# Layer 1's keys written by tile in the projection, a late end of attention blocks, and result stores from GpSimd

## The chip, the cores and the metric

The kernel runs on one core of a Trainium2 chip, as one launch. The metric is the device time of that launch in microseconds (us). A core has five engines with in-order instruction streams: TensorE (PE in the profile; its weight loads are listed as PEld), VectorE (DVE), ScalarE (ACT), GpSimd (POOL) and SyncE (SP, which here only issues transfers). A transfer is issued by an engine's queue and carried out by the core's 16 DMA engines.

## The reference

A backbone of two layers over 2048 latent tokens (a grid of 32 rows by 64 columns) of width 1024, with 256 context tokens. All is float32. Layer 0 mixes multi-head latent attention and a gated linear attention and updates both streams; layer 1, which the change is about, is a 2-D neighbourhood attention with 16 heads of 64:

```python
def odd_mixer(h, hc, w_in, q_gain, k_gain, rpb, w_out, update_ctx):
    ...                                   # q, k, v, z = split(h @ w_in); q, k = rms_norm per head
    o = neighborhood_attention(q_x, k_x, v_x, k_c, v_c, rpb)
    y = jnp.dot(o.reshape(...) * jax.nn.silu(z_x), w_out)

def neighborhood_attention(q, k, v, k_ctx, v_ctx, rpb):
    # a query at (row, col) sees a window of 8 rows x 16 columns of latent keys, with a bias
    # by relative place, and all 256 context keys
    s_lat = einsum('bqhd,brkhd->bhqrk', qr, kb) * scale + bias      # masked outside the 16 columns
    s_ctx = einsum('bqhd,bchd->bhqc', qr, k_ctx) * scale
    p = softmax(concatenate([s_lat, s_ctx], axis=-1))
    return p[..., :n] @ vb + p[..., n:] @ v_ctx
```

Each layer ends with `x = x + gate * y`. Products are kept near float32 accuracy by splitting an operand into a high part (type fp32r, which the fast matmul takes) and a low part.

## The kernel before

The work goes through stages one after the other: layer 0's projections, its attentions, its output projection, then layer 1: `odd_qk` (query and key projections), `odd_vz` (value and gate projections, woven with row maxima of the scores), `odd_attention`, and the output projection. Intermediate tensors (Q1, K1, V1, z1, RT1) go to device memory and come back. Instructions are written in program order; a scheduler of the tile framework then orders them on each engine by its own model of time, and `tc.issue_after(x)` adds the constraint that what is issued in its scope comes after x. A tile name with `bufs=n` is a ring of n buffers: the next use of a buffer waits until all readers of the last one are done.

*`odd_qk`.* A `cell` is one 128-token tile times 512 columns: 24 matmuls, the sum of squares, the power by POOL (`rpow`, L197), and the scaling. Its second half, `fin`, runs inside the next cell: four PE transposes (L1133), ACT writes the high part `oqh` (L106 is the helper of all activations), DVE the low part `oql` (L1137), and SP stores both to Q1 or K1 with tokens in row order (L1143). Of a key cell, both parts go to K1.

*`odd_attention`* runs over eight pairs of heads j. A pair goes through 20 steps: c0, c1, l0 to l3, c2, l4 to l7, c3, l8 to l15. A "c" step takes the 256 context keys against 512 queries; an "l" step takes one tile of 128 keys (8 rows by 16 columns) against its rectangle of queries. Four l steps form a group g, which covers 512 keys. A step is:

- the scores: two accumulating matmuls per head and key tile, `scores` (L1321 and L1322). The second one has 65 rows: 64 of the keys' high part against the queries' low part, and a row of ones against the row maxima;
- for l steps, DVE adds the bias table into a probability tile `opt` (L1431); ACT takes the exponential;
- two steps later in a batch of two (the list `pend`), the *tail*: P·V into the block's PSUM tile `o` (L1348 for c, L1363 for l), and the running sums of probabilities `oacc`: DVE adds the two context halves (L1354), POOL adds l tiles (L1371).

The latent queries form four blocks of 512. After steps 7, 11 and 15 the tail ends blocks 0, 1, and 2 with 3: `finish` (L823 to L837) sums `oacc` over partitions with two matmuls (L828) into a PSUM tile of the scores' own ring "st" of four, ACT takes a logarithm and an exponential for the reciprocal, DVE refines it (L833, L834) and multiplies it with `o` (L835), POOL multiplies with the gate `ozt` (L836), and SP stores the result to RT1 (L837). `finish` serves layer 0's attention too.

*Loads.* All are on SP's queue. Per pair: queries (L1281 to L1283, six of 512 KB and two short ones), context keys `kc`, values (L1309 for context, L1311 for eight parts of V1 in rows of 512 bytes), two bias tables (L1316). Per group, `keys` loads 512 keys into the staging tile `kb` (one buffer), 64 partitions at a time: high and low part stacked on 128 partitions (L1293), the high part again (L1294), and a row of ones (L1295). The generator `by_tile` then copies `kb` to `kt` with ACT, from rows of the grid to tiles of 16 columns, 128x512 and 65x512 for each head; one such copy is issued after the last exponential of each l step of the group before. The rings: `st` 4 and `o` 4 in PSUM, `opt` 10, `kt` 2, queries 2.

In the last pair the output weights are loaded and split in the places that queries, values, tables and keys leave (`weights`).

## Time and profile before

| | us |
|---|---|
| median of 3 runs | 3788.31 |
| the three runs | 3780.18, 3788.31, 3790.68 |
| profiled execution | 3781.03 |
| its span in the trace | 3779.2 |
| `odd_qk` | 2205 to 2655 |
| `odd_vz` and row maxima | 2655 to 3111 |
| `odd_attention` | 3111 to 3592 |
| layer 1's output projection | 3592 to 3779 |

All durations are from the profiled execution. Its page gives the busy time of each engine, and the granted clock of TensorE as a mean, 0.979 over the span. A row of a window gives the busy time and, in brackets, the number of instructions that began in it. A row of the timeline gives start, duration, engine, line, operation, output and input, and in square brackets how long the engine had been idle and which other instruction it waited for; "SPq" is the issue of a transfer by SyncE. In a row of the waits the columns are the total, the number and the longest wait. A few per cent of the matmuls can be missing from a trace.

### The profile page before, as it was taken

What the parts mean: (1) busy time and instruction counts of PE and PEld (TensorE: products, weight loads), DVE (VectorE), ACT (ScalarE), POOL (GpSimd) and SP (SyncE); (2) the same over time, 40 slices, a digit from 0 to 9 for tenths busy, and PEclk for the clock granted to TensorE, in tenths of its full rate; (3) what the DMA queues carried; (4) which work ended last, traced back from release to release, by engine and by line L of the source; (5) the groups of instructions that cost most, each with busy time, mean ns of one, the idle gap of its engine ahead of it and who ended that gap; (6) DMA issues with size and microseconds to landing.
All of it is one profiled execution on the core that took longest, in us unless ns stands there. A gap on an engine that the chain in (4) does not pass through costs nothing. (4 is left out here: it accounts for less than half of the span.)

```text
span 3779.2 us, 52751 instructions
## 1 busy us (share of the span) xinstructions
PE 3608.8 (95%) x18404; PEld 2768.6 (73%) x18404; DVE 2368.2 (63%) x4699; ACT 1474.2 (39%) x2932; POOL 1418.8 (38%) x1585
## 2 busy tenths in 40 slices
PE   7999989999999999989999999998999998889899
PEld 6988978888876666645557878887888875545577
DVE  4677656888866666696654344445687745657732
ACT  4445541111135555545552133334222225656610
POOL 1434320010024444445642223333444426766722
PEclk9999999999999999999999999999999998899999
DMA  7455453222252331425515544446444459787543
GB/s 253 138 165 163 130 169 97 70 86 70 76 134 67 85 98 58 115 78 146 144 37 184 162 136 132 128 133 184 152 137 146 118 142 199 197 192 184 158 143 117
DMA packets 373820, 503.03 MB, mean 133 GB/s; under 512 B 29554, under 2 KB 250834, under 8 KB 367651
## 3 DMA queue, kind: packets, MB, share of 16 engines
q1 hardware_dynamic: 339122, 443.55, 41.9%
q0 software_dynamic: 11776, 28.13, 2.4%
q10 hardware_dynamic: 22656, 27.99, 2.1%
q8 instruction: 146, 2.39, 0.3%
q14 instruction: 120, 0.98, 0.1%
HBM read 329.60 MB, written 169.93 MB: 132 GB/s over the span
## 5 line engine op out<-in xcount | busy, mean ns | idle before, releaser
L106 ACT ACTIVATE apt<-st 128x512 f32<-128x512 f32 (+1 forms) x592 | 343.4, 593 | 278.5 <-PE st L963 248.4
L647 DVE TENSOR_REDUCE mm<-mx 128x1 f32<-128x512 f32 (+1 forms) x656 | 389.0, 627 | 82.2 <-PE mx L646 75.1
L952 DVE TENSOR_TENSOR acc<-acc,apt 128x512 f32<-128x512 f32 x288 | 272.9, 971 | 143.2 <-ACT apt L106 141.7
L952 POOL TENSOR_TENSOR acc<-acc,apt 128x512 f32<-128x512 f32 x160 | 227.5, 1435 | 188.8 <-ACT apt L106 188.1
L1371 POOL TENSOR_TENSOR oacc<-oacc,opt 128x341 f32<-128x341 f32 (+7 forms) x336 | 238.7, 742 | 115.3 <-ACT opt L106 80.1
L893 PE MATMUL av<-apt,av 128*64 128x512 f32 (+1 forms) x1184 | 279.1, 595 | 0.1
L961 PE MATMUL st<-aq,akh 97*128 97x512 f32 (+1 forms) x592 | 255.1, 431 | 8.3 <-ACT apt L106 6.2
L646 PE MATMUL mx<-mk,mq 96*128 96x512 f32 (+1 forms) x656 | 236.7, 373 | 6.2 <-DMA mq<-QT 4.7
L962 PE MATMUL st<-aq,akh 96*128 96x512 f32 (+1 forms) x592 | 233.5, 395 | 0.0
L963 PE MATMUL st<-aq,akl 96*128 96x512 f32 (+1 forms) x592 | 232.9, 394 | 0.0
L1239 DVE CUSTOM_DVE_ANT_1 mx<-mx,mtab 128x225 f32<-128x225 f32 (+13 forms) x576 | 183.6, 339 | 58.6 <-PE mx L1233 43.2
L106 ACT ACTIVATE u<-gm 128x352 f32<-128x352 f32 (+1 forms) x140 | 68.7, 498 | 370.2 <-PE gm L125 208.7
L1075 POOL TENSOR_TENSOR px<-py,px 128x512 f32<-128x512 f32 x68 | 89.8, 1321 | 277.0 <-DVE py L1074 274.8
L893 PEld LDWEIGHTS av<-apt,av 128*64 128x64 f32 x1184 | 80.4, 137 | 153.3 <-issue 151.5
L1431 DVE TENSOR_TENSOR opt<-st,tab 128x64 f32<-128x64 f32 (+10 forms) x576 | 144.9, 313 | 70.0 <-PE st L1322 50.5
L1074 DVE TENSOR_TENSOR py<-pj,gate 128x512 f32<-128x512 f32 x68 | 46.9, 690 | 217.6 <-PE pj L116 217.6
L961 PEld LDWEIGHTS st<-aq,akh 97*128 97x128 f32 x592 | 111.8, 189 | 96.0 <-issue 46.8
L106 ACT ACTIVATE opt<-opt 128x465 f32<-128x465 f32 (+7 forms) x256 | 123.0, 497 | 57.0 <-DVE opt L1431 47.3
L646 PEld LDWEIGHTS mx<-mk,mq 96*128 96x128 f32 x656 | 121.7, 189 | 17.7 <-issue 5.1
L106 ACT ACTIVATE prh<-pr 128x1024 fp32r<-128x1024 f32 x34 | 35.7, 1056 | 251.6 <-PE pj L115 251.6
L1321 PE MATMUL st<-q,kt 128*128 128x480 f32 (+5 forms) x256 | 100.9, 404 | 34.4 <-ACT opt L106 17.3
L963 PEld LDWEIGHTS st<-aq,akl 96*128 96x128 f32 x592 | 112.8, 191 | 25.2
(436 smaller groups left out, 10314.4 us busy)
## 6 DMA issues: line engine op xcount, KB each, us to landing
q<-Q SPq DMA_DIRECT2D x48, 512.0 KB
kb<-K SPq DMA_DIRECT2D x192, 128.0 KB
H<-x ACTq DMA_DIRECT2D x36, 512.0 KB
pr<-RT SPq DMA_DIRECT2D x34, 512.0 KB
adaw<-ada_w SPq DMA_DIRECT2D x64, 256.0 KB
x<-H SPq DMA_DIRECT2D x32, 512.0 KB
wraw<-w_od SPq DMA_DIRECT2D x64, 256.0 KB
mtab<-rpb_q SPq DMA_DIRECT2D x16, 899.0 KB
```

Source lines behind the costliest of these rows:

```text
L106: return self.nc.scalar.activation(out, in_, func, **kw)
L646: mm = nc.tensor.matmul(ps[:, :w], q[:A_QK, (t % 6) * P : (t % 6) * P + P], k[:A_QK, k0 : k0 + w], start=True, stop=True)
L647: nc.vector.tensor_reduce(out=m[:, t, n : n + 1], in_=ps[:, :w], axis=AX.X, op=ALU.max)
L893: nc.tensor.matmul(O[j, nb][i * 64 : i * 64 + 64, :w], V[j, kt // TT][:, kt % TT, i * 64 : i * 64 + 64], pts[i][:, :w], start=n == 0, stop ...
L952: eng.tensor_tensor(out=acc[i][e][:, :w], in0=a[:, :w], in1=pts[i][:, :w], op=ALU.add)
L961: nc.tensor.matmul(ps[:, :w], kh[: A_QK + 1, i, kq], qh[: A_QK + 1, :w], start=True, stop=False)
L962: nc.tensor.matmul(ps[:, :w], kh[:A_QK, i, kq], ql[:A_QK, :w], start=False, stop=False)
L963: mm = nc.tensor.matmul(ps[:, :w], kl[:A_QK, i, kq], qh[:A_QK, :w], start=False, stop=True)
L1239: nc.vector.tensor_tensor_reduce(out=s, in0=s, in1=tb[:, ri : ri + rn, ci : ci + cn], scale=1.0, scalar=-3e38, op0=ALU.add, op1=ALU.max, a ...
L1321: nc.tensor.matmul(ps, k1, q1, start=True, stop=False)
L1371: eng.tensor_tensor(out=a, in0=a, in1=pts[i][:, a0 - r0 : a1 - r0, :], op=ALU.add)
L1431: nc.vector.tensor_tensor(out=pt[:, d[0], d[1]], in0=ps[:, d[0], d[1]], in1=tabs[i][:, ri : ri + rn, ci : ci + cn], op=ALU.add)
```

## The change

It changes what `odd_qk` stores, what `odd_attention` loads, and when and by which engine some of the work is issued. The matmuls are the same in number and shape.

1. *Keys by tile.* K1 now holds only the high part in row order (the row maxima still read it), so 36 stores of low parts go away. Of latent keys `fin` also writes high and low part in tile order: ACT and DVE, for each of the two grid rows of a token tile, into SBUF tiles `okt` that collect four token tiles (512 keys). The ACT copy of 256 elements a partition comes on top of `oqh` (64 more in all), and two DVE instructions of 256 replace one `oql` of 512 (32 replaced by 64). `store_k` writes a full group to a new tensor K1t (pair, head, 64 rows high and 64 low, token) with four POOL transfers: 32 in all, with rows of 2 KB, and 16 for the context keys.
2. *Direct load.* `keys` loads a group straight to `kt1` (one transfer for 128 partitions and both heads) and `kt2` (one for 64 partitions). The row of ones of `kt2` and `kc2` is set once by POOL. The staging tile, `by_tile`'s 128 ACT copies, and the transfers of the rows of ones are gone. `kt1` and `kt2` are rings of two, so the load for group g+1 can be issued when the scores of group g-1 are done.
3. *Context sums.* The two context parts of a head lie in one `opt` tile of 2 x 512 (five buffers instead of ten of 512), and one `tensor_reduce` with a strided view adds them instead of a `tensor_tensor`.
4. *Block ends.* `finish` writes DVE's first step into the PSUM tile `den` in place, and L834 reads it there; the log tile `rl` and `rc` have 2 and 3 buffers in layer 1. A block's end is put in a list `late` and issued two batches of tails later (the second of two blocks three). Its result is stored from POOL's queue.
5. *Prefetch.* What pair 1 loads is issued after the key load in pair 0's second group; the output weights' steps come after the last key load. The pools on the right side are allocated in another order, with one more (`lp`).

In the scheduled order of the changed kernel, TensorE's instructions up to the end of `odd_vz` are in the same order but for two groups in layer 0's attention. On SyncE, pair 0's queries, keys, mask and tables now stand ahead of the load of the context values (L1309 in the kernel before), and the eight loads of V1 come last. The scores that take over a denominators' PSUM tile wait for L834 instead of L833.

```diff
@@ -820,21 +820,21 @@
...
-    def finish(self, av, dacc, zt, dst, w, ap, pp, tag):
+    def finish(self, av, dacc, zt, dst, w, ap, pp, tag, lnp=None, bufs=(1, 2), out=None):
 
         nc = self.nc
...
-        ln = self.tl(ap, [P, 512], "rl", bufs=1)
-        rc = self.tl(ap, [P, 512], "rc", bufs=2)
+        ln = self.tl(lnp or ap, [P, 512], "rl", bufs=bufs[0])
+        rc = self.tl(ap, [P, 512], "rc", bufs=bufs[1])
         self.act(ln[:, :w], den[:, :w], AF.Ln, scale=-1.0)
         self.act(rc[:, :w], ln[:, :w], AF.Exp, scale=-1.0)
-        nc.vector.tensor_tensor(out=ln[:, :w], in0=den[:, :w], in1=rc[:, :w], op=ALU.mult)
-        nc.vector.scalar_tensor_tensor(out=rc[:, :w], in0=ln[:, :w], scalar=2.0, in1=rc[:, :w], op0=ALU.add, op1=ALU.mult)
+        nc.vector.tensor_tensor(out=den[:, :w], in0=den[:, :w], in1=rc[:, :w], op=ALU.mult)
+        nc.vector.scalar_tensor_tensor(out=rc[:, :w], in0=den[:, :w], scalar=2.0, in1=rc[:, :w], op0=ALU.add, op1=ALU.mult)
         nc.vector.tensor_tensor(out=rc[:, :w], in0=av, in1=rc[:, :w], op=ALU.mult)
         nc.gpsimd.tensor_tensor(out=rc[:, :w], in0=rc[:, :w], in1=zt, op=ALU.mult)
-        nc.sync.dma_start(dst, rc[:, :w])
+        (out or nc.sync).dma_start(dst, rc[:, :w])
...
@@ -1091,7 +1091,8 @@
...
-        self.K1 = self.scr("K1", (2, 8, P, T), F32)
+        self.K1 = self.scr("K1", (8, P, T), F32)
+        self.K1t = self.scr("K1t", (8, 2, P, T), F32)
...
@@ -1132,14 +1133,39 @@
...
                 hi = self.tl(sp, [P, 4, P], "oqh", F32R)
-                lo = self.tl(sp, [P, 4, P], "oql", F32R)
                 self.act(hi[:], ps[:], AF.Copy, scale=qkg[:, z : z + 1])
-                nc.vector.scalar_tensor_tensor(out=lo[:], in0=ps[:], scalar=qkg[:, z : z + 1], in1=hi[:],
-                                               op0=ALU.mult, op1=ALU.subtract)
-                dst, o = (self.Q1, (t - NCT) * P) if z == 0 else (self.K1, t * P)
                 j0 = (j % 2) * 4
-                for part, tt in enumerate((hi, lo)):
-                    nc.sync.dma_start(dst[part][j0 : j0 + 4, :, o : o + P].rearrange("j p t -> p j t"), tt[:].bitcast(F32))
+                if z == 1:
+                    nc.sync.dma_start(self.K1[j0 : j0 + 4, :, t * P : t * P + P].rearrange("j p t -> p j t"), hi[:].bitcast(F32))
+                if z == 0 or t < NCT:
+                    lo = self.tl(sp, [P, 4, P], "oql", F32R)
+                    nc.vector.scalar_tensor_tensor(out=lo[:], in0=ps[:], scalar=qkg[:, z : z + 1], in1=hi[:],
+                                                   op0=ALU.mult, op1=ALU.subtract)
+                    if z == 0:
+                        for part, tt in enumerate((hi, lo)):
+                            nc.sync.dma_start(self.Q1[part][j0 : j0 + 4, :, (t - NCT) * P : (t - NCT) * P + P].rearrange("j p t -> p j t"),
+                                              tt[:].bitcast(F32))
+                    else:
+                        store_k((hi, lo), j0, t * P, P)
+                    return
+                g, r0 = divmod(2 * (t - NCT), 8)
+                if r0 == 0:
+                    kt[j] = [self.tl(sp, [P, 4, 512], f"okt{j}{part}", F32R, bufs=1) for part in range(2)]
+                view = lambda x, n: x[:].rearrange("p i (r c b) -> p i r c b", r=n, c=4)
+                for r in range(2):
+                    oh, ol = (x[:].rearrange("p i (c r b) -> p i r c b", c=4, r=8)[:, :, r0 + r] for x in kt[j])
+                    self.act(oh, view(ps, 2)[:, :, r], AF.Copy, scale=qkg[:, z : z + 1])
+                    nc.vector.scalar_tensor_tensor(out=ol, in0=view(ps, 2)[:, :, r], scalar=qkg[:, z : z + 1],
+                                                   in1=view(hi, 2)[:, :, r], op0=ALU.mult, op1=ALU.subtract)
+                if r0 == 6:
+                    store_k(kt.pop(j), j0, CTX + g * 512, 512)
+
+            def store_k(parts, j0, o, w):
+
+                for u, x in enumerate(parts):
+                    for i in range(2):
+                        nc.gpsimd.dma_start(self.K1t[j0 : j0 + 4, i, u * 64 : u * 64 + 64, o : o + w].rearrange("j d t -> d j t"),
+                                            x[i * 64 : i * 64 + 64].bitcast(F32))
...
@@ -1284,24 +1310,19 @@
...
-            def keys(j, c0, w, tag, bufs=2):
-                k1 = self.tl(ap, [P, 2, w], tag + "1", F32R, bufs=bufs)
-                k2 = self.tl(ap, [P, 2, w], tag + "2", F32R, bufs=bufs)
-                for i in range(2):
-                    b = i * 64
-                    for u in range(2):
-                        nc.sync.dma_start(k1[u * 64 : u * 64 + 64, i].bitcast(F32), self.K1[u, j, b : b + 64, c0 : c0 + w])
-                    nc.sync.dma_start(k2[:64, i].bitcast(F32), self.K1[0, j, b : b + 64, c0 : c0 + w])
-                    nc.sync.dma_start(k2[64:65, i].bitcast(F32), self.KT[0, 0, A_QK : A_QK + 1, :w])
+            ones = {"kc": [self.tl(ap, [P, 2, CTX], f"kc2{n}", F32R, bufs=1) for n in range(2)],
+                    "kt": [self.tl(kp, [P, 2, 512], f"kt2{n}", F32R, bufs=1) for n in range(2)]}
+            for x in ones["kc"] + ones["kt"]:
+                nc.gpsimd.memset(x[64:65].bitcast(F32), 1.0)
+
+            def keys(j, c0, w, pool, tag):
+
+                k1 = self.tl(pool, [P, 2, w], tag + "1", F32R, bufs=len(ones[tag]))
+                nc.sync.dma_start(k1[:].bitcast(F32), self.K1t[j, :, :, c0 : c0 + w].rearrange("i d t -> d i t"))
+                k2 = ones[tag].pop(0)
+                ones[tag].append(k2)
+                self.kload = nc.sync.dma_start(k2[:64].bitcast(F32), self.K1t[j, :, :64, c0 : c0 + w].rearrange("i d t -> d i t"))
                 return k1, k2
-
-            def by_tile(k, out):
-                for z, n in enumerate((P, 65)):
-                    o = self.tl(kp, [P, 2, 512], f"kt{z}", F32R)
-                    out.append(o)
-                    for i in range(2):
-                        self.by_tile(o[:n, i], k[z][:n, i].bitcast(F32))
-                        yield
...
@@ -1322,22 +1343,21 @@
...
-            pend = []
+            pend, late = [], []
...
+                with self.tc.issue_after(start.ins) if j == 1 else ExitStack():
+                    Q = queries(j)
+                    kc = keys(j, 0, CTX, ap, "kc")
+                    if j == 0:
+                        kt = [keys(0, CTX, 512, kp, "kt")]
+                    else:
+                        V = values(j)
...
+                    tabs = [table(2 * j + i, i) for i in range(2)]
+                    if j == 0:
+                        V = values(j)
...
@@ -1345,13 +1365,13 @@
...
-                        nc.vector.tensor_tensor(out=a, in0=pts[i][0][:], in1=pts[i][1][:], op=ALU.add)
+                        nc.vector.tensor_reduce(out=a, in_=pts[i][:].rearrange("p u c -> p c u"), axis=AX.X, op=ALU.add)
...
@@ -1369,12 +1389,14 @@
...
-                    for bb in done:
-                        zt = self.tl(fp, [P, 512], "ozt")
-                        nc.sync.dma_start(zt[:], self.z1[j, :, bb * 512 : bb * 512 + 512])
-                        a = [acc[bb // 2, i][:].rearrange("p r c -> p (r c)")[:, (bb % 2) * 512 : (bb % 2) * 512 + 512] for i in range(2)]
-                        self.finish(O.pop(bb)[:].rearrange("p r c -> p (r c)"), a, zt[:],
-                                    self.RT1[j, :, bb * 512 : bb * 512 + 512], 512, fp, pp, ("st", 4))
+                    late.extend([2 + u, finish_block, bb, j, O, acc] for u, bb in enumerate(done))
+
+                def finish_block(bb, j, O, acc):
+                    zt = self.tl(fp, [P, 512], "ozt", bufs=3)
+                    nc.sync.dma_start(zt[:], self.z1[j, :, bb * 512 : bb * 512 + 512])
+                    a = [acc[bb // 2, i][:].rearrange("p r c -> p (r c)")[:, (bb % 2) * 512 : (bb % 2) * 512 + 512] for i in range(2)]
+                    self.finish(O.pop(bb)[:].rearrange("p r c -> p (r c)"), a, zt[:],
+                                self.RT1[j, :, bb * 512 : bb * 512 + 512], 512, fp, pp, ("st", 4), lp, (2, 3), nc.gpsimd)
...
@@ -1390,7 +1412,7 @@
...
-                            pl = [self.tl(kp, [P, 2, 512], f"kt{z}", F32R)[:].rearrange("p i c -> p (i c)") for z in range(2)]
+                            pl = [self.tl(kp, [P, 2, 512], "kt1", F32R, bufs=2)[:].rearrange("p i c -> p (i c)") for z in range(2)]
...
@@ -1398,29 +1420,27 @@
...
-                    pts = []
                     g, c = divmod(n, 4)
+                    exps = lambda: self.tl(ep, [P, 2, 512], "opt", bufs=5)
+                    pts = exps() if kind == "l" else [exps(), exps()]
                     if kind == "l" and c == 0 and (j, g) != (7, 3):
-                        kt.append([])
-                        nxt = by_tile(keys(j + (g == 3), CTX + (g + 1) % 4 * 512, 512, "kb", 1), kt[1])
+                        kt.append(keys(j + (g == 3), CTX + (g + 1) % 4 * 512, 512, kp, "kt"))
+                        if (j, g) == (0, 1):
+                            start = self.kload
...
-                                self.act(pt[:], ps[:], AF.Exp)
-                                pts[i].append(pt)
+                                self.act(pts[i][:, u, :], ps[:], AF.Exp)
...
@@ -1430,33 +1450,39 @@
...
-                        last = self.act(pt, pt, AF.Exp)
-                        pts.append(pt)
-                    if kind == "l":
-                        with self.tc.issue_after(last.ins):
-                            next(nxt, None)
+                        self.act(pt, pt, AF.Exp)
                     if kind == "l" and c == 3:
                         kt.pop(0)
+                    if kind == "l":
+                        pts = [pts[:, i, : nr * w].rearrange("p (r c) -> p r c", r=nr) for i in range(2)]
...
                     if len(pend) == 4:
                         with self.tc.issue_after(mm.ins):
                             for f, *a in pend[:2]:
                                 f(*a)
+                            for x in late:
+                                x[0] -= 1
+                                if x[0] <= 0:
+                                    x[1](*x[2:])
+                        late[:] = [x for x in late if x[0] > 0]
                         del pend[:2]
                     if j == 7 and kind == "l" and n % 2:
-                        next(out_w)
-                        if n == 15:
-                            next(out_w, None)
-                            yield
+                        with self.tc.issue_after(self.kload.ins):
+                            next(out_w)
+                            if n == 15:
+                                next(out_w, None)
+                                yield
...
+            for _, f, *a in late:
+                f(*a)
...
-            qb, kp, qa, tp, vp = [self.pool(es, "oa" + n, bufs=2, side="right", reuse_waits="tile") for n in ("QB", "KT", "QA", "T", "V")]
+            qb, vp, lp, qa, kp, tp = [self.pool(es, "oa" + n, bufs=2, side="right", reuse_waits="tile") for n in ("QB", "V", "L", "QA", "KT", "T")]
```

32 lines of the change are left out of this document (9 added, 23 removed).

## The prediction

> **What bounds the kernel now.** I read the page first, then the windows of the stages, then windows of 10 us inside the last attention, then its timeline and its table of waits. The page says that TensorE is the bound almost everywhere. The windows by stage (columns: stretch, length, then busy time and instructions of PE, PEld, DVE, ACT, POOL, then granted clock, DMA share, GB/s) say where it is not:
>
> ```profile
> PE 3608.8 (95%) x18404; PEld 2768.6 (73%) x18404; DVE 2368.2 (63%) x4699; ACT 1474.2 (39%) x2932; POOL 1418.8 (38%) x1585
> ...
> 2205.00:2655.00 450.00, 437.62 (x2097) 360.61 (x2096) 216.72 (x335) 174.35 (x344) 143.53 (x175) 0.99 0.50 150
> 2655.00:3124.00 469.00, 449.42 (x2201) 374.76 (x2199) 325.91 (x1358) 118.59 (x195) 182.20 (x158) 0.99 0.47 137
> 3124.00:3592.00 468.00, 414.38 (x2433) 242.28 (x2434) 309.45 (x794) 287.84 (x590) 316.79 (x382) 0.93 0.78 185
> ```
>
> The q/k stage (2205 to 2655) has PE idle for 12 us at full clock. Layer 1's attention (3124 to 3592) has 54 us of PE idle and a clock of 0.93. No other engine is near its limit there (POOL 68%), but DMA is at 0.78. So whatever the change can bring lies in that stage and at its door.
>
> The door (timeline: start, duration, engine, line, idle before it and releaser):
>
> ```profile
> 3110.60 0.39 PE L125 MATMUL gm<-w1h,hlo 128*128 128x512 f32 x1
> ...
> 3111.49 1.25 SPq L1309 DMA_DIRECT2D ov<-V1c  x2
> ...
> 3116.85 1.34 SPq L1281 DMA_DIRECT2D q<-Q  x2
> ...
> 3124.84 1.19 PE L1321 MATMUL st<-q,kc 128*128 128x512 f32 x2 [13.86 <-DMA q<-Q]
> ...
> 3132.88 0.63 PE L1322 MATMUL st<-q,kc 65*128 65x512 f32 x1
> ...
> 3135.68 1.98 PE L1348 MATMUL o<-opt,ov 128*64 128x512 f32 x4
> 3190.81 0.38 PE L1363 MATMUL o<-opt,ov 128*64 128x124 f32 x4
> 3191.12 0.50 PE L1321 MATMUL st<-q,kc 128*128 128x512 f32 x1
> ...
> 3548.01 0.50 PE L1321 MATMUL st<-q,kc 128*128 128x512 f32 x1
> ```
>
> The projection ends at 3111.0; PE then waits 13.9 us for queries, which SyncE issues only behind the value load at L1309, and the first P·V matmul (L1348) runs at 3135.7. The last rows are the starts of head pairs 1 and 7: 356.9 us apart, 59.5 us a pair. Pair 7, which loads no next pair, takes 44.0 us to 3592. So 59.5 is not PE's own work. The next rows show a whole pair, and then its windows of 10 us:
>
> ```profile
> 3250.40:3309.50 59.10, 52.21 (x304) 30.53 (x303) 36.32 (x98) 34.73 (x72) 38.09 (x48) 0.91 0.83 193
> 3309.50:3368.00 58.50, 51.84 (x299) 29.05 (x299) 35.22 (x97) 33.70 (x70) 36.92 (x48) 0.94 0.80 185
> ...
> 3260.00:3270.00 10.00, 7.39 (x52) 5.28 (x48) 1.07 (x4) 3.07 (x6) 3.19 (x6) 0.94 1.00 232
> 3270.00:3280.00 10.00, 7.50 (x31) 4.08 (x29) 3.49 (x8) 6.11 (x13) 6.11 (x9) 0.55 0.91 225
> ...
> 3300.00:3310.00 10.00, 9.46 (x38) 3.98 (x36) 7.67 (x19) 5.12 (x10) 4.05 (x5) 1.00 1.02 226
> ...
> 3380.00:3390.00 10.00, 7.52 (x54) 4.99 (x50) 1.38 (x5) 3.07 (x6) 3.88 (x7) 1.00 0.91 226
> 3390.00:3400.00 10.00, 7.91 (x30) 4.26 (x30) 5.64 (x8) 6.38 (x14) 6.97 (x8) 0.66 0.82 223
> ```
>
> Once a pair PE, ACT and DVE all stop, and PE then works at 0.55 of its clock. The timeline of one such place and the waits of the stage give the cause:
>
> ```profile
> 3259.22 2.37 SPq L1293 DMA_DIRECT2D kb<-K  x4
> ...
> 3265.56 0.63 ACT L106 ACTIVATE kt<-kb 128x512 fp32r<-128x512 f32 x1 [8.65 <-DMA kb<-K]
> ...
> 3266.34 0.45 SPq L1294 DMA_DIRECT2D kb<-K  x1
> ...
> 3266.72 3.67 PE L1363 MATMUL o<-opt,ov 128*64 128x93 f32 x24 [2.40 <-ACT opt L106]
> ...
> 3270.93 0.63 ACT L106 ACTIVATE kt<-kb 65x512 fp32r<-65x512 f32 x1 [2.29 <-DMA kb<-K]
> ...
> 3272.47 0.67 PE L1321 MATMUL st<-q,kt 128*128 128x360 f32 x1 [2.08 <-ACT opt L106]
> ```
>
> ```profile
> ACT kt L106 <- DMA kb<-K: 61.2, 17, 8.6
> ...
> PE st L1321 <- ACT opt L106: 18.1, 16, 3.1
> ...
> PE st L1321 <- DMA q<-Q: 13.9, 1, 13.9
> ...
> PE o L1363 <- ACT opt L106: 9.1, 7, 2.4
> ...
> PE st L1321 <- DVE rl L833: 3.1, 6, 0.6
> ```
>
> ACT's queue is in order. The copy that puts keys in tile order (kt<-kb) stands in it ahead of exponentials, and waits 61.2 us in all for key loads that came 6.3 us (3259.2 to 3265.6) after their issue. The exponentials behind it, and PE behind them, wait too: PE is named 18.1 + 9.1 us behind ACT.
>
> **The change, part by part.** The durations:
>
> ```profile
> L106 ACT ACTIVATE kt<-kb 65x512 fp32r<-65x512 f32 (+1 forms) x128 | 79.2, 619 | 64.0 <-DMA kb<-K 61.2 <-DMA kb<-KT 2.6
> ...
> L1354 DVE TENSOR_TENSOR oacc<-opt,opt 128x512 f32<-128x512 f32 x64 | 60.8, 971 | 101.4 <-ACT opt L106 100.8
> ...
> L834 DVE SCALAR_TENSOR_TENSOR rc<-rl,rc 128x512 f32<-128x512 f32 x30 | 34.3, 1142 | 0.7
> ...
> L835 DVE TENSOR_TENSOR rc<-o,rc 128x512 f32<-128x512 f32 x30 | 20.4, 681 | 0.4
> ...
> L197 POOL TENSOR_TENSOR oss<-oss,mhalf 128x8 f32<-128x8 f32 x68 | 112.6, 1656 | 5.5
> ...
> L1228 DVE TENSOR_REDUCE mm<-mx 128x2 f32<-128x512 f32 x128 | 88.2, 689 | 34.2 <-PE mx L1226 33.4
> ...
> L1137 DVE SCALAR_TENSOR_TENSOR oql<-tp,oqkg,oqh 128x512 fp32r<-128x512 f32 x68 | 50.9, 748 | 23.9 <-ACT oqh L106 23.9
> ...
> L1163 POOL DMA_DIRECT2D V<-ovz x60 | 33.3, 558 | 127.5 <-ACT ovz L106 127.3 <-issue 0.2
> ```
>
> 1. *Key copies removed.* The 128 copies leave ACT (79.2 us), and with them the place where ACT waits for keys. Keys now go straight into a ring of two, so a load is due a whole group of four tiles later. A group is a quarter of a pair, some 11 to 15 us (44.0/4, 59.5/4), against a landing of 6.3 us. Per pair the loss is PE's idle time plus its slow time. Window 3260 to 3280: idle 2.61 + 2.50, slow 7.50 x 0.45 + 7.39 x 0.06 = 3.8, together 8.9. Window 3380 to 3400: 2.48 + 2.09 + 7.91 x 0.34 = 7.3. Mean 8.1. What is late next is the key load itself, since a pair's DMA work is 0.83 x 59.1 = 49 us or 0.80 x 58.5 = 47 us whatever ACT does. I take 7.3 back of 8.1, a pair of about 52 us, three above DMA's work. Six pairs have the dip (pair 0 has the door instead): **-44 us**. Ends: 0 (keys as late as ever) and -75 (a pair at DMA's 47).
>
> The Trainium skill (TensorE: Matmul & The Clock Gate, Part 1) has the clock throttled by default and released after about 3.4 us of work. By that the slow part of a dip would be worth 3.4/2 = 1.7 us, and the step -36 instead of -44; the trace shows longer slow stretches, 3124.8 to past 3132.9 at the door.
>
> 2. *The door.* The new order on SyncE puts queries, keys and tables ahead of the value load that waits for V's writes. The scores can start when the projection ends; the tails still want V, whose nine loads come last. They are 1.2 MB, 5 us at the 232 GB/s of the windows above, and land some 6 us after their issue at 3111.5, so L1348 moves from 3135.7 to about 3123: **-12 us** (ends -4, if V comes as late as the queries did, and -14, the whole wait for q).
>
> 3. *Context sums* become one strided reduce over 1024 elements. Twice the 689 ns of the reduce of 512 gives 1.38, against 0.97: 64 x 0.41 = 26 us more on DVE (ends: -18 at 0.69, +84 at twice L834's 1.14). The division read from PSUM (L834, 1.14) falls at best to the 0.75 of L1137, which reads PSUM: -13 us. DVE has 309 us of 468, so its cover is 150 us; **0**. Without the cover half of the 13 us would show.
>
> 4. *Block ends late, results from POOL.* Scores and denominators share four PSUM banks. Until now a denominator's bank came free at L833, and PE waited for that six times, 3.1 us; now it is held through L834, 0.75 to 1.14 us longer, 32 times. In the new order some 26 matmuls stand between a second block's denominators and the score that reuses their bank: 26 x 0.21 us = 5.5 (437.62/2097 a matmul). The chain is 2 x 0.62 (ACT, by the copy's row) + 0.68 + 1.14 = 3.1 without queueing, so it is covered in most blocks. I take nine waits longer by 0.75: +7; the wait of the old order for the last sums falls with the later start: -4. Together **+3** (ends -7 and +36, 32 x 1.14). 32 result DMAs move past SyncE to POOL: 32 x 0.56 = 18 us there, on top of 317 of 468, with bias tables and sums queued behind; 335 of 418 is 80%: **0**, and 18 without that cover.
>
> 5. *The q/k stage.* The low key parts go (32 of L1137, -24 us DVE), 64 half-size ones and 64 ACT copies come (DVE at most 48, ACT at most 64 x 0.62 = 40 against 276 free). SyncE loses 36 stores; POOL gains 48 (48 x 0.56 = 27 us, with 306 free) in 12 bursts of four, 2.2 us each. Behind a burst on POOL wait the two L197 of a cell, for which the transposes wait; these are woven one cell later, 24 x 0.21 = 5.0 us of PE work, so a burst is covered: **+3** for those that aren't. Ends 0 and 27. The order of PE's matmuls is unchanged in this stage.
>
> Sum: -44 - 12 + 3 + 3 = -50 us. Against the profiled execution's 3781.0 (span 3779.2) that is 3731. The execution lay 7.3 us under the median, so on the median's footing 3738.
>
> **Rivals.**
> *A, keys late in the burst.* The first 20 to 30 us of a pair carry the next pair's queries, tables and values at 225 to 232 GB/s and share 0.91 to 1.02. If the key load queues behind these, PE waits for it directly, again at 0.55 clock. For it: DMA's 47 to 49 us leave little room in 52. Against it: 11 us of lead. A pair of 57 us: 6 x 2.5 + 12 - 6 = 21, so 3767. The Trainium skill (DMA: Bandwidth & Descriptors, Issuing engines are not separate DMA queues) speaks for it: moving results to POOL frees no transfer time, as all queues interleave on the same 16 engines.
> *B, more.* Nothing is left but DMA: a pair of 47.5 us and a full door give 6 x 12 + 14 = 86, so 3702. Pair 7's 44.0 us speaks for it; the smaller idles in good windows (0.54 in 3300 to 3310) against.
> *C, the other side: the denominators' bank.* The 3.1 us chain of step 4 starts on ACT, whose queue may hold up to eight exponentials of the next context steps (some 0.6 each). If four stand ahead, the 2.4 us of slack are gone, and every further microsecond is PE's, four blocks a pair. It decides against the change from 50/32 = 1.6 us a block past the cover, a chain of 7.1. At 2.5 a block: 3738 + 32 x 2.5 = 3818. For it: ACT's queue is where PE waits now. Against it: the waits for this bank so far are 0.6 at most.
> *D, nothing moves:* the dip is DMA's alone and the door as late, 3788; or A with an uncovered q/k stage, 3767 + 24 = 3791.
>
> **How the numbers follow.** Forecast 0.50 (own range 3720 to 3755), A 0.18, B 0.12, D 0.07, C 0.13. Below 0.3% (11 us) a measurement of this kernel can't tell a difference. Faster 0.80, same 0.07, slower 0.13. From 3695 (B with a little more) to 3785 (A up to nearly nothing) lies 0.8 of it.
>
> **What would show it.** Right: no wait of ACT for key loads; windows of the attention without a clock under 0.9; pair starts 52 us apart; first P·V matmul some 12 us after the projection. Step 1 is wrong if PE's table of waits names key loads; step 3 if DVE's reduce is over 2 us and PE's scores wait for DVE; step 4 if PE's scores wait for L834 by more than 10 us in all, or L828 for POOL; step 5 if the q/k stage grows past 455 us. A DMA share above 0.95 over a whole pair would make A's case.

## The result, and the profile after

The changed kernel takes 3765.86 us (median of 4 runs, 3760.43 to 3770.8) against 3789.49 us (4 runs, 3780.18 to 3791.56): a ratio of 0.9946, 95% interval 0.9932 to 0.9959. The gain is 23.6 us where 50 were forecast; the time lies outside the forecast's own range (3720 to 3755) and inside the wide one (3695 to 3785). The profiled executions differ by 15.7 us (spans 3763.5 and 3779.2), and the readings below add up to that.

The page of the changed kernel, its first lines:

```profile
span 3763.5 us, 52191 instructions
...
PE 3585.0 (95%) x18404; PEld 2760.9 (73%) x18404; DVE 2373.4 (63%) x4731; ACT 1441.5 (38%) x2868; POOL 1436.7 (38%) x1669
```

The stages as windows (stretch, length, busy time and instructions of PE, PEld, DVE, ACT, POOL, granted clock, DMA share, GB/s). The changed kernel: the q/k stage, the v/z stage, pair 0, pair 1, pairs 2 to 6, pair 7 up to the output projection, and the rest:

```profile
2201.40:2671.10 469.70, 454.33 (x2158) 374.16 (x2157) 224.08 (x369) 198.67 (x411) 179.93 (x226) 0.98 0.56 168
2671.10:3119.90 448.80, 441.05 (x2164) 367.79 (x2163) 330.88 (x1360) 118.05 (x194) 180.93 (x159) 1.00 0.44 133
3119.90:3179.80 59.90, 45.86 (x280) 28.33 (x278) 31.63 (x89) 24.76 (x51) 27.37 (x37) 0.89 1.02 203
3179.80:3240.00 60.20, 49.39 (x307) 31.10 (x306) 37.64 (x98) 28.68 (x56) 45.17 (x61) 0.86 0.78 185
3240.00:3506.20 266.20, 238.91 (x1522) 142.69 (x1520) 187.39 (x490) 140.54 (x280) 190.06 (x261) 0.94 0.91 206
3506.20:3572.60 66.40, 52.44 (x331) 31.36 (x329) 50.60 (x119) 38.14 (x76) 43.82 (x59) 0.90 0.56 162
3572.60:3763.50 190.90, 181.77 (x768) 144.70 (x768) 60.42 (x53) 18.94 (x20) 43.90 (x35) 0.97 0.41 131
```

The same landmarks in the kernel before:

```profile
2199.40:2662.50 463.10, 450.72 (x2154) 371.34 (x2154) 219.72 (x339) 178.42 (x350) 151.25 (x180) 0.99 0.50 153
2662.50:3110.60 448.10, 441.54 (x2169) 368.60 (x2167) 325.91 (x1358) 115.60 (x191) 175.25 (x153) 1.00 0.45 130
3110.60:3172.90 62.30, 46.74 (x282) 30.11 (x280) 30.84 (x90) 33.56 (x69) 36.21 (x44) 0.81 0.85 193
3172.90:3235.40 62.50, 52.41 (x306) 30.30 (x304) 40.48 (x100) 37.01 (x76) 41.22 (x49) 0.92 0.90 211
3235.40:3529.10 293.70, 263.57 (x1522) 151.25 (x1520) 187.81 (x492) 174.26 (x361) 196.11 (x241) 0.94 0.81 189
3529.10:3591.90 62.80, 51.95 (x331) 30.52 (x329) 50.21 (x117) 43.52 (x88) 43.78 (x52) 0.97 0.52 151
3591.90:3779.20 187.30, 180.60 (x768) 144.92 (x768) 61.92 (x55) 18.06 (x19) 43.60 (x34) 0.99 0.42 131
```

Row by row, the differences are +2.0 (start of the q/k stage), +6.6, +0.7, -2.4, -2.3, -27.5, +3.6 and +3.6: -15.7. The attention gains only in its middle. Five pairs go from 58.7 to 53.2 us each, pairs 0 and 1 hardly move, pair 7 and the end lose, and the stages ahead of the attention give 9 us back.

The door of the changed kernel (timeline):

```profile
3119.89 0.39 PE L125 MATMUL gm<-w1h,hlo 128*128 128x512 f32 x1
...
3120.12 1.35 PE L1342 MATMUL st<-q,kc 128*128 128x512 f32 x4
...
3131.08 6.34 PE L1368 MATMUL o<-opt,ov 128*64 128x512 f32 x16 [4.64 <-DMA ov<-V1c]
```

The scores start as the projection's last matmul ends (PE waited 13.9 us there before), and the first P·V matmul (L1368 now) comes 10.8 us after that end (24.7 before).

The waits of the attention (engine, line, what was waited for: total, times, longest):

```profile
ACT opt L106 <- DVE opt L1451: 141.6, 104, 7.3
...
POOL tab L1338 <- DMA tab<-rpb_k: 66.3, 9, 12.3
...
PE st L1342 <- DVE opt L1451: 15.5, 27, 2.4
PE st L1342 <- DMA kt<-K1t: 15.4, 5, 6.0
...
PE pj L114 <- ACT prh L106: 9.1, 1, 9.1
PE st L1342 <- DVE rc L834: 8.9, 2, 8.4
```

ACT no longer waits for keys; PE itself does, 15.4 us. New is one long wait for L834 (8.4 us, in pair 1), and the wait ahead of the output projection has grown from 3.4 to 9.1 us.

### The profile page after: what moved, and what is told of

Read it like the earlier page. It is cut to its first block, busy times and chain, and to the rows that moved or that the text cites. A ratio compares the mean times of both kernels' runs of the same rounds, so it can differ in the third digit from the quotient of the medians.

```text
span 3763.5 us, 52191 instructions
## 1 busy us (share of the span) xinstructions
PE 3585.0 (95%) x18404; PEld 2760.9 (73%) x18404; DVE 2373.4 (63%) x4731; ACT 1441.5 (38%) x2868; POOL 1436.7 (38%) x1669
## 4 chain that ended last, share of the span: by engine, by line
PE 74%; DMA 12%; DVE 6%; issue 3%; POOL 3%; ACT 2%; SPq 0%; POOLq 0%; ACTq 0%; DVEq 0%
PE gm L123 9%; PE gm L124 9%; PE gm L125 9%; PE av L893 6%; PE st L961 4%; PE mx L646 4%; PE pj L116 3%; PE pj L114 3%; PE pj L115 3%; PE st L962 3%; PE st L963 3%; DMA q<-Q 2%; DMA wraw<-w_od 2%; DMA ov<-V 1%; DMA kt<-K1t 1%
## 5 line engine op out<-in xcount | busy, mean ns | idle before, releaser
L1391 POOL TENSOR_TENSOR oacc<-oacc,opt 128x341 f32<-128x341 f32 (+6 forms) x336 | 213.3, 664 | 47.0 <-ACT opt L106 39.9
L962 PEld LDWEIGHTS st<-aq,akh 96*128 96x128 f32 x592 | 113.3, 191 | 16.9
```

What stands on the lines that cost most here:

```text
L962: nc.tensor.matmul(ps[:, :w], kh[:A_QK, i, kq], ql[:A_QK, :w], start=False, stop=False)
L1391: eng.tensor_tensor(out=a, in0=a, in1=pts[i][:, a0 - r0 : a1 - r0, :], op=ALU.add)
```

## The experiments

All ratios are to the kernel before, run on the same chip. "Five pairs" is the stretch from pair 2's first scores to pair 7's, as in the windows above (293.7 before, 266.2 in the change).

**Each part of the change alone, or left out.** The key layout with the direct load, without the rest:

```diff
-                    late.extend([2 + u, finish_block, bb, j, O, acc] for u, bb in enumerate(done))
+                    for bb in done:
+                        finish_block(bb, j, O, acc)
-                                ... ("st", 4), lp, (2, 3), nc.gpsimd)
+                                ... ("st", 4), lp, (2, 3), nc.sync)
-                with self.tc.issue_after(start.ins) if j == 1 else ExitStack():
+                with ExitStack():
...
-                        nc.vector.tensor_reduce(...)
+                        nc.vector.tensor_tensor(out=a, in0=pts[i][:, 0, :], in1=pts[i][:, 1, :], op=ALU.add)
```

(and the output weights' steps not held back)

> The keys by tile and their direct load alone (parts 1 and 2 of the change); the context sums, the block ends, SyncE's stores, the prefetch and the place of the weights as before; the buffers of the rings as in the changed kernel. Theory: all of the gain is in parts 1 and 2, and the rest of the change costs more than it gives: 3750 to 3760, below the changed kernel. Rival: the keys alone give a part only, and the later prefetch or the late ends give the rest: 3770 to 3785.

Measured: 1.0043 (1.0031 to 1.0056). The window of its five pairs, one key load in its timeline with the wait for it, and its waits:

```profile
3241.00:3534.60 293.60, 250.31 (x1523) 151.18 (x1521) 185.23 (x494) 137.81 (x280) 188.31 (x241) 0.92 0.80 187
```

```profile
3327.29 0.37 SPq L1321 DMA_DIRECT2D kt<-K1t  x1
...
3336.21 0.64 PE L1342 MATMUL st<-q,kt 128*128 128x360 f32 x1 [7.19 <-DMA kt<-K1t]
```

```profile
PE st L1342 <- DMA kt<-K1t: 34.7, 6, 7.2
```

Removing the 128 copies brings nothing in these pairs: 293.6 against 293.7. SyncE sends the third key group 27.6 us after the pair's start (3299.7), behind the next pair's queries, values and tables, and it lands 8.9 us later. PE waits six times for key loads, 34.7 us in all and 7.2 us at this place. This is rival A's mechanism. That the kernel as a whole is slower than before goes with its q/k and v/z stages, which take some 14 us longer.

The block ends at once again, the rest as changed (stores on SyncE), and the same with the stores left on POOL:

```diff
-                    late.extend([2 + u, finish_block, bb, j, O, acc] for u, bb in enumerate(done))
+                    for bb in done:
+                        finish_block(bb, j, O, acc)
```

> The changed kernel with block ends at once, in the tail that completes the block, and the results stored by SyncE as before. Theory: the late ends and POOL's stores are what lets PE wait 9.1 us before the output projection (3.4 before), so undoing them gives 4 to 6 us back at the end, and the middle of the attention stays as it is: about 3761. Rival: the late ends take waits for the denominators out of the pairs, and undoing them costs 2 us a pair: about 3778. No effect at all, 3766, would say that both are small or cancel.

> The changed kernel with block ends at once in the tail that completes the block, and POOL's stores kept. Theory S (SyncE's stores hold up the keys): stays at 0.994 to 0.997 of before. Theory L (the lateness of the ends counts): 1.000 to 1.004, with PE waiting 25 us or more for key loads. Both in part: 0.998 to 1.000.

Measured: 1.0042 (1.0028 to 1.0055) and 1.0075 (1.0063 to 1.0088). So the late ends are worth 1.0% in the changed kernel: all of the gain, and more. The first of these once more:

> The kernel with the block ends at once, one more look for its rows (ratio 1.004).

gave 3800.04 us in one execution (1.0054). In each of pairs 2 to 6 PE waits once for keys, 7.1 to 9.1 us.

Late ends alone, put into the kernel before:

> The kernel before, with only the block ends issued two and three batches of tails later; SyncE's stores, the rings, keys, sums and prefetch as before. In the changed kernel the late ends alone are worth 1.0% of before (ratio 0.9945 with, 1.004 without). Theory M: a late end finds both heads' sums ready, so that its two denominators' matmuls run side by side on TensorE (57 us busy in the 128 records of L828 before, 35 after), and PE no longer stops for sums; that needs no other key layout. Then L828 falls to 35 to 45 us here too and the time by 15 to 30 us: ratio 0.992 to 0.996. Rival: in the kernel before, ScalarE's wait for keys comes at the same place and eats it: 0.998 to 1.002.

Measured: 1.0003 (0.9994 to 1.0012), nothing. There ACT waits for keys 47.8 us instead of 63.8, but PE's wait for ACT's exponentials doubles, from 18.1 to 37.5 us. The denominators' matmuls (L828) do fall there, from 57.0 to 42.0 us busy, as theory M has it, but the time does not follow. The gain of the late ends needs the copies gone, and the gain of the copies' removal needs the late ends.

The stores alone: back to SyncE in the changed kernel, and to POOL in the kernel before.

```diff
-        nc.sync.dma_start(dst, rc[:, :w])
+        (out or nc.sync).dma_start(dst, rc[:, :w])      # out = nc.gpsimd in layer 1
```

> The changed kernel, late ends kept, with the results stored by SyncE as before. Undoing both the late ends and POOL's stores made it 1.0% slower, with PE waiting 6 us a pair for a key load that stands on SyncE behind two result stores and their gate loads. Theory S: the stores in SyncE's in-order queue do that, as each waits for POOL's last product: with them back on SyncE the kernel loses most of the 1.0%, ratio to before 1.000 to 1.004, PE waiting 25 us or more for key loads. Theory L: it is the ends at once that did it (their gate loads and waits ahead of the key load): then late ends alone keep the gain, ratio 0.994 to 0.996.

> The kernel before, with only the result stores of layer 1 moved from SyncE to POOL. Theory S: there too the key loads, and behind them ScalarE's copies, wait behind the stores: 8 to 20 us faster, ratio 0.995 to 0.998, and ScalarE's wait for keys falls from 61 us to under 40. Theory L, or keys late for another reason (the values' transfers ahead of them): 0.999 to 1.001 with the wait unchanged. If POOL's queue is hurt by the stores: above 1.001.

Measured: 0.9945 (0.9932 to 0.9957), no difference from the change; and 1.0068 (1.0055 to 1.008), 0.7% slower. The waits of the kernel before with its stores on POOL:

```profile
PE st L1321 <- ACT opt L106: 30.9, 18, 5.0
DVE rl L833 <- ACT rc L106: 20.1, 12, 4.0
ACT rc L106 <- DMA RT<-rc: 13.9, 5, 3.9
```

ACT waits until the block's result has left `rc`, DVE waits for ACT, and PE for the exponentials behind it. With three `rc` buffers one such wait of 2.6 us is left in the change, and none with the ends at once and the stores on POOL (1.0075); what costs 0.3% there is not shown.

The context sums as before, and pair 1's loads not held back (all of them, or its queries alone released earlier, by pair 0's last value load):

```diff
-                        nc.vector.tensor_reduce(out=a, in_=pts[i][:].rearrange("p u c -> p c u"), axis=AX.X, op=ALU.add)
+                        nc.vector.tensor_tensor(out=a, in0=pts[i][:, 0, :], in1=pts[i][:, 1, :], op=ALU.add)
```

> The changed kernel with the context sums by the two-operand add again (64 instructions, on the same tiles). Theory: the strided reduce takes 1.24 us against 0.97, 17 us of VectorE's time that lies beside other work: 3766 within 4 us. Rival: VectorE's in-order queue is where the exponentials wait now (141.6 us of ScalarE's waits name its bias adds), and 0.3 to 0.5 us more or less in each of 64 places, 8 a pair, shows: 3755 to 3760 with the add.

```diff
-                with self.tc.issue_after(start.ins) if j == 1 else ExitStack():
+                with ExitStack():
```

> The changed kernel, but what pair 1 loads is no longer held back until the key load of pair 0's second group. Theory: the held-back loads are what made pairs 0 and 1 of layer 1's attention slow (59.7 and 60.2 us, where pairs 2 to 6 took 53.2 on average), through a key load that PE waited for (6.0 us) and bias tables that came 12 us late. Then pair 1 takes about 53 us, pair 0 about 55, and the time falls by some 10 us to about 3756. Rival: pair 1's queries now stand on SyncE ahead of pair 0's context keys and values, so that the first P.V matmul comes 10 us later: 3766 or more, no gain. A second rival: the slow pairs are the start of DMA's load as such, whatever its order: 3766, pairs 0 and 1 at 120 us together.

> The changed kernel, with pair 1's queries released by the last value load of pair 0 instead of the key load of pair 0's second group; the other loads of pair 1 as in the change. Releasing all of pair 1's loads at once took pairs 0 and 1 from 119.9 to 104.2 us, but lost 4 us each at the projection's end and at the context keys. Theory: SyncE idles 7 us between the value load and the key load, and this order keeps the door as in the change (scores at the projection's end, P.V 11 us later) and shortens pairs 0 and 1 to 108 to 114: 6 to 12 us faster than the changed kernel, ratio to before 0.991 to 0.993. Rival: the key load of the third group now queues behind 3 MB of queries and PE waits for it in pair 0: pairs 0 and 1 together 118 or more, ratio 0.994 to 0.996.

Measured: 0.9946 (0.9932 to 0.996), 0.9940 (0.9923 to 0.9957) and 0.9957 (0.9943 to 0.9971); none can be told from the change. Without the hold, pairs 0 and 1 take 104.2 us instead of 119.9, but the v/z stage grows by 6 us and the first scores wait 4.2 us for keys.

**What the late ends do.** The denominators of a block's two heads (L828) go to two halves of the array's columns. One block in the change (four records, 1.03 us) and one before (twice two records) with the groups of L828 in each, then the group of L828 in the changed kernel with the two heads' matmuls held apart (`half_block` and `finish_block` as two late steps):

```profile
3336.26 1.03 PE L828 MATMUL st<-oacc,mtwos 128*64 128x512 f32 x4
...
L828 PE MATMUL st<-oacc,mtwos 128*64 128x512 f32 x128 | 34.8, 595 | 4.5 <-POOL oacc L1391 3.1 <-DMA kt<-K1t 1.3
```

```profile
3280.03 1.02 PE L828 MATMUL st<-oacc,mtwos 128*64 128x512 f32 x2
...
3282.08 1.07 PE L828 MATMUL st<-oacc,mtwos 128*64 128x512 f32 x2
...
L828 PE MATMUL st<-oacc,mtwos 128*64 128x512 f32 x128 | 57.0, 609 | 2.1 <-POOL oacc L1371 1.4 <-ACT opt L106 0.6
...
PEld st L828 <- POOL oacc L1371: 7.6, 15, 1.4
```

```profile
L828 PE MATMUL st<-oacc,mtwos 128*64 128x512 f32 x128 | 65.5, 601 | 10.8 <-DVE opt L1457 7.1 <-POOL oacc L1393 3.6
```

> The changed kernel, ends late as in the change, but the two denominators' matmuls of a block held apart by the P.V matmuls of a tail (8 to 14 matmuls between them, 1 in the changed kernel). Nothing else is made earlier or later by more than one batch. Theory M: the pairs no longer run side by side, L828 rises from 35 to 57 us or more and the time by 15 to 25 us: ratio to before 0.999 to 1.001. Rival: side by side or not is worth nothing, the lateness itself (POOL's and DVE's sums done before PE asks) is: 0.994 to 0.997.

Measured: 0.9976 (0.9966 to 0.9985), 0.3% or 11 us slower than the change (0.9946). Before, 12 of the 32 blocks have two to six records of scores between the two heads' matmuls, as in the block shown. Of the other 20, 16 take 1.45 to 2.3 us, and PE's weight loads for L828 wait 15 times for POOL's sums. In the change 31 blocks have nothing between, and 29 of these take 1.03 to 1.08 us. Held apart, with 14 to 24 records of P·V between the heads in 30 blocks, they cost 0.3%; P·V also goes to halves of the columns, so part of the 65.5 us may overlap it. Undoing the late ends with the stores on POOL costs 1.3% (1.0075), so running side by side is about a quarter of their worth; in it are waits ahead of L828, which rise from 4.5 to 10.8 us.

Which blocks have to be late (stores on SyncE; only the end of the second half's blocks, or only the first half's, in `late`):

```diff
+                    if n == 15:        # the other run: if n < 15
                         late.extend([2 + u, finish_block, bb, j, O, acc] for u, bb in enumerate(done))
+                    else:
+                        for bb in done:
+                            finish_block(bb, j, O, acc)
```

> The changed kernel with results on SyncE (0.9945 of before), and only the ends of a pair's last two blocks late; blocks 0 and 1 end at once. All four at once gave 1.004. Theory P (phases): a pair has a first part of 36 us that DMA sets (share 1.07) and in which PE waits for keys, and a second part that PE sets; a late end of blocks 2 and 3 moves their denominators and the waits for their sums out of the second part into the first of the next pair, where they cost nothing. Then this kernel has most of the gain: 0.995 to 0.998, second part (third key group to next pair) under 20 us instead of 22 to 23. Rival (side by side): the gain is that the halves of the denominators run together; blocks 0 and 1 have the widest gaps between their halves, so they hold most of it: 1.000 to 1.003.

> The same with blocks 0 and 1 late and blocks 2 and 3 at once; the halves of all denominators stand next to each other in PE's order. Theory P: the second part keeps the ends of blocks 2 and 3: 0.999 to 1.003. Rival (side by side): most of the gain, 0.995 to 0.998, with L828 under 45 us.

Measured: 1.0053 (1.004 to 1.0067) and 0.9988 (0.9978 to 0.9998). Blocks 2 and 3, whose ends move across the pair's boundary, bring nothing by themselves; blocks 0 and 1 bring 0.54%; both together 0.97% (against 1.0042). The parts don't add, and neither forecast holds. With blocks 2 and 3 late the second part of a pair takes 24.4 us on average, where theory P had under 20. With blocks 0 and 1 late L828 is at 35.2 us, as in the change, yet the kernel is 0.4% slower than with all ends late: side by side alone does not give the rest. PE's waits for keys fall there to one of 4.3 us, but it waits 47.0 us for VectorE's `opt` instead.

The bank of the denominators (step 4), freed one instruction earlier by writing `ln` instead of `den`:

```diff
-        nc.vector.tensor_tensor(out=den[:, :w], in0=den[:, :w], in1=rc[:, :w], op=ALU.mult)
-        nc.vector.scalar_tensor_tensor(out=rc[:, :w], in0=den[:, :w], ...)
+        nc.vector.tensor_tensor(out=ln[:, :w], in0=den[:, :w], in1=rc[:, :w], op=ALU.mult)
+        nc.vector.scalar_tensor_tensor(out=rc[:, :w], in0=ln[:, :w], ...)
```

> The changed kernel, in which the second to last step of the block end writes SBUF (ln) and not the denominators' bank in place, so that the bank comes free one instruction earlier and L834 reads SBUF. Step 4 of the prediction (bank held through L834, +7 us over 29 block ends): the ratio falls by about 0.0015 to 0.002, to 0.993, L834 falls from 677 ns. Rival: the bank isn't what the block ends cost once they are late (the waits for L834 are 8.9 us in two places): within 0.001 of the change, 0.9946.

Measured: 0.9948 (0.9929 to 0.9967). The bank doesn't cost what step 4 put down. L834 takes the same from either source: in the change, and here (20 of the 52 are layer 0's). In the kernel before it also read SBUF and took 1.14 us on average; why is not shown.

```profile
L834 DVE SCALAR_TENSOR_TENSOR rc<-st,rc x32: 668/676/691, 3173.7 to 3569.2; 128x512 f32<-128x512 f32 x32
```

```profile
L834 DVE SCALAR_TENSOR_TENSOR rc<-rl,rc x52: 410/682/1902, 1123.3 to 3562.2; 128x512 f32<-128x512 f32 x48, 128x256 f32<-128x256 f32 x4
```

**What sets the first part of a pair.** From a pair's first scores to those of its third key group pass, on average over the five pairs, 36.5 us before the change, 35.1 in it and 36.6 with the key layout alone, with DMA at a share of 0.9 to 1.1. The tables of pairs 1 to 7 left out (two of 128x1034 a pair, 1.06 MB):

```diff
-                    tabs = [table(2 * j + i, i) for i in range(2)]
+                    tabs = [table(2 * j + i, i) for i in range(2)] if j == 0 else tabs
```

> The changed kernel without the bias tables of pairs 1 to 7 (their loads, 1.06 MB a pair, and their mask additions on POOL are left out, pair 0's tables are used for all). Theory T (in the first 36 us of a pair the transfers are the bound: DMA share 1.07, and keys and tables share the queues): this stretch shrinks by several us a pair, pairs 2 to 6 fall from 53.2 to under 50, and the whole by 20 us or more (ratio under 0.989). Rival C (the copies on ScalarE and the half clock after stalls set the pair): pairs 2 to 6 stay at 52 to 53.5, and only pairs 0 and 1 lose their 12 us wait for tables (ratio 0.991 to 0.9946).

Measured: 0.9899 (0.9881 to 0.9916). Pairs 0 and 1 fall from 119.9 to 105.5 us, but the five pairs only from 266.2 to 261.3. The first part of pair 3 in the change (the window runs 1.1 us past it) and without tables, then that of pair 4 in each:

```profile
3291.50:3327.50 36.00, 31.71 (x184) 18.18 (x182) 24.62 (x55) 19.68 (x39) 22.92 (x27) 0.95 1.07 240
```

```profile
3278.70:3314.70 36.00, 29.25 (x183) 17.41 (x181) 24.54 (x55) 19.57 (x39) 22.96 (x33) 0.96 1.09 202
```

```profile
3344.00:3381.20 37.20, 29.59 (x182) 17.05 (x181) 24.63 (x55) 19.66 (x39) 23.93 (x29) 0.97 1.08 222
```

```profile
3333.90:3365.60 31.70, 29.21 (x182) 17.36 (x181) 24.53 (x55) 19.57 (x39) 22.30 (x32) 1.00 1.08 225
```

Pair 3 does not shorten (34.9 and 36.0 us), but it is the exception: without tables the other four take 31.7 to 33.8 us, and the mean of the five falls from 35.1 to 33.1, with about 12% fewer bytes moved in it by the rows of the five. What follows in a pair grows from 18.1 to 19.1. So the first part follows the amount loaded, as theory T has it, but by 2 us a pair and not by several, and half of it is lost again behind; most of this kernel's gain lies in pairs 0 and 1, as rival C has it. The share stays at 1.06 to 1.09 with the tables and without: it doesn't tell how much there is to load.

Then the place in SyncE's queue: the values of pairs 2 to 7 issued behind the fourth key group, not ahead of the third. Two rows first, the third group's issue in the change (27 us after the pair's start) and what PE waits at it:

```profile
3318.43 0.38 SPq L1321 DMA_DIRECT2D kt<-K1t  x1
...
3326.40 0.40 PE L1342 MATMUL st<-q,kt 128*128 128x360 f32 x1 [0.98 <-DMA kt<-K1t]
```

```diff
                         kt.append(keys(j + (g == 3), CTX + (g + 1) % 4 * 512, 512, kp, "kt"))
+                        if g == 2:
+                            third = self.kload
...
-                        V = values(j)
+                        with self.tc.issue_after(third.ins) if j > 1 else ExitStack():
+                            V = values(j)
```

> The changed kernel, in which the values of pairs 2 to 7 are loaded after the fourth key group of the pair before, not ahead of its third. Theory Q (SyncE's queue: the third key group goes out 27 us after the pair's start, behind the next pair's queries, tables and values, and lands 9 us later beside them, and that sets the first 36 us of each pair): the third group goes out and lands some 4 us earlier, PE's waits for keys (15.4 us) fall under 6 us, the first part of a pair falls from 36 to 32 or 33 us, pairs 2 to 6 from 53.2 to about 51, ratio 0.990 to 0.992. Rival C (the key group's buffer comes free only then, or ScalarE and VectorE set the pair): first part 36 us, pairs 2 to 6 at 53, ratio 0.994 to 0.996.

Measured: 0.9949 (0.9936 to 0.9961), no gain. Its third group's issue (pair 3 starts at 3300.2), its five pairs, and its waits:

```profile
3315.06 0.39 SPq L1321 DMA_DIRECT2D kt<-K1t  x1
```

```profile
3245.90:3510.90 265.00, 238.14 (x1523) 144.15 (x1521) 186.60 (x490) 139.02 (x281) 189.32 (x260) 0.94 0.90 208
```

```profile
DVE opt L1454 <- POOL oacc L1392: 37.8, 16, 6.9
...
PE st L1342 <- DVE opt L1454: 26.2, 30, 5.0
...
PE st L1342 <- DMA kt<-K1t: 4.5, 1, 4.5
```

The group leaves 12 us earlier and the wait for it is gone from every pair but pair 0. In its place PE waits for VectorE's `opt` (26.2 us, up to 5.0, instead of 15.5), and VectorE for POOL's sums, which read `opt`. The third group's scores still start 34.9 us into pair 3 (3335.10 after 3300.2; in the change 3326.40 after 3291.5), and on average over the five pairs at 36.6 us, not at theory Q's 32 to 33. I read it so: once the ends are late, the keys are only one of two waits that end at about the same time.

**A better version.** The change with pair 1's loads not held, stores on SyncE with four `rc` buffers, and output weights not held; and the same with the values late:

```diff
-                with self.tc.issue_after(start.ins) if j == 1 else ExitStack():
+                with ExitStack():
-                                ... lp, (2, 3), nc.gpsimd)
+                                ... lp, (2, 4), nc.sync)
-                        with self.tc.issue_after(self.kload.ins):
-                            next(out_w)
+                        next(out_w)
```

> The changed kernel with pair 1's loads not held back, the results on SyncE with a ring of four for them, and the output weights not held back until the last key load. Theory: the 15 us that pairs 0 and 1 lose and 3 to 5 us of the wait before the output projection come back, less 6 us at the projection's end: 3740 to 3750 where before is 3779, ratio 0.990 to 0.992. Rival: what one place gains the next gives back, because DMA's work sets the first 36 us of every pair: 0.993 to 0.996.

> The variant with early loads of pair 1, stores on SyncE, a ring of four and weights not held, and the values of pairs 2 to 7 loaded late as well. Theory Q: 0.988 to 0.990, below the 0.9924 without it. Rival C: 0.992 to 0.993.

Measured: 0.9924 (0.9912 to 0.9936), 3750.13 us, and 0.9955 (0.9938 to 0.9973). The first beats the kernel before, and the change by 0.2%, where the two intervals just meet. Late values cost it 0.3%: its five pairs go from 260.0 to 274.6 us.

## Why the prediction was wrong

**What bounds the kernel.** Right about the stage, wrong about pairs. The rows quoted as starts of pairs 1 and 7 (3191.12, 3548.01) are scores of a later context step, some 18 us into the pair. The period of 59.5 us is right all the same, since both are the same step, but pair 7 runs from 3529.1 to 3591.9, 62.8 us, not 44.0. So "59.5 is not PE's own work" had lost this piece of evidence, and rival B its own. Pair 1 did have a dip, but the hold on its loads kept it from gaining, so five pairs could gain, not six.

**Step 1 (-44) failed**: "I take 7.3 back of 8.1". Taking out the copies alone gives 0 in five pairs. The forecast compared a lead of 11 to 15 us with a landing of 6.3 us, as if the load left as soon as its buffer was free. But SyncE sends the third group behind the next pair's loads, 27 us into the pair (14.9 us with the values out of its way, with the same ring of two), and it lands 8 to 9 us later. ACT's wait became PE's.

**Step 2 (-12)** was right about the door, not about the time: the first P·V came 13.9 us earlier, but the stretch to pair 1 shortened by only 2.4. The prefetch held back goes with this: the tables come late (the 12.3 us wait of L1338), and without the hold pairs 0 and 1 take 15.7 us less.

**Step 3 (0)** was right: without the strided sum the time is the same. The reduce takes less than the 1.38 put down, a row of the change:

```profile
L1374 DVE TENSOR_REDUCE oacc<-opt x64: 1217/1236/1262, 3122.9 to 3539.4; 128x512 f32<-128x1024 f32 x64
```

**Step 4 (+3) failed in sign and size.** It priced the bank (+7), the wait for the last sums (-4) and the stores (0), and nothing else that a late end moves. The late ends are worth -1.0%, some 36 us. In the profiled executions, the change has its five pairs 27.4 us shorter than the key layout alone has: 11.4 in PE's busy time and 16.0 in idle time. The side-by-side denominators are 15.4 of busy time (L828 alone in both windows, PE's busy time and PEld's ahead of the clock; key layout alone, then the change):

```profile
3241.00:3534.60 293.60, 36.03 (x80) 8.74 (x80) 0.92 0.80 187
```

```profile
3240.00:3506.20 266.20, 20.58 (x82) 5.31 (x80) 0.94 0.91 206
```

The waits for keys are 20.5 less in these windows (29.9 and 9.4 us), other waits 4.5 more. By place, 1.5 us a pair are gained up to the third key group's scores (36.6 to 35.1) and 4.0 behind them (22.1 to 18.1), so what the waits for keys lose is not simply the time gained. Why late ends shorten these waits is not settled: the later half of the blocks alone leaves them at 38.6 us over the whole attention, the earlier half alone takes them away but puts waits for `opt` there, and with the keys sent early in the change the time stays. Blocks ended at once together with the keys sent early were not tried. The bank of rival C decided once, in pair 1:

```profile
3202.57 2.36 POOL L1338 TENSOR_TENSOR tab<-tab,maskk 128x1034 f32<-128x1034 f32 x1 [7.46 <-DMA tab<-rpb_k]
...
3208.89 1.23 DVE L1391 TENSOR_TENSOR oacc<-oacc,opt 128x372 f32<-128x372 f32 x1 [8.21 <-POOL oacc L1391]
...
3210.05 0.68 DVE L834 SCALAR_TENSOR_TENSOR rc<-st,rc 128x512 f32<-128x512 f32 x1
...
3210.78 0.80 PE L1342 MATMUL st<-q,kc 128*128 128x512 f32 x1 [8.38 <-DVE rc L834]
```

Its cause was not ACT's queue: POOL waited for a bias table, a sum on VectorE (L1391) waited for POOL, and L834 stood behind that sum. The 0 for the stores held with the ends late; with the ends at once POOL's queue costs 0.3% here and 0.7% in the kernel before.

The Trainium skill (DMA: Bandwidth & Descriptors, Issuing engines are not separate DMA queues) has moving a DMA to another engine save only the sequencer's issue time. The trace agrees where the ends are late (0.9945 and 0.9946) and adds that it can cost: 0.7% in the kernel before, where ACT waited 13.9 us for the stored buffer.

**Step 5 (+3)** had the right sign, and +6.6 lies within its ends of 0 and 27, but it is over twice the term and past the prediction's own sign of being wrong (450 growing past 455). All kernels with keys by tile have this stage at 466 to 472 us. Of the 6.6, 3.0 are PE's idle time (12.4 to 15.4); which of the added work makes it was not tested.

**Not priced at all:** the prefetch held back and the weights' place. The end loses 3.6 us in pair 7 and 3.6 in the output projection; PE's wait ahead of it goes from 3.4 to 9.1 us. That the variant without these holds is the fastest complete kernel fits, but it changes four things at once, and their shares were not measured one by one.

**Rivals and chances.** A came true as to its mechanism (PE waits for the keys directly) and its time (3767 against 3765.9), but by another sum, so the match in time is luck: the pairs gained what A denied them through the late ends, and the kernel lost time at the end of the attention, behind it and ahead of it. That the five pairs came to 53.2 us, near the 52 of step 1, is luck too, as the late ends and not the copies brought them there.

## What to carry to other kernels

A wait in front of an engine is worth its length only if what it waits for can come sooner: before removing the instruction that waits, follow the transfer back to its place in the issuing queue and to the buffer that it needs. Price every part of a change against what the other parts leave; here two parts brought nothing alone, and 0.5% of the kernel before together. And before a stretch is measured from one row to the end of a stage, check which step of the loop the row is: two rows of the same step gave the period rightly, but the last pair's length was counted from its middle. The same care holds for a pair that is to stand for all: look at every one of them.
